# First stage of a hybrid encoder: the order of loads and stores on the sync queue around the memory's weights

## The chip, the core and the metric

The kernel is one program on one NeuronCore of a Trainium2 chip. The metric is the device time of one execution in microseconds (us). TensorE (PE) multiplies, VectorE (DVE), ScalarE (ACT) and GpSimd (POOL) do the rest, and all loads and stores are issued by SyncE (SP), one after the other, in one queue. SP's instructions are transfers ("DMA"), which run on 16 DMA engines.

## What is computed

One encoder layer over two sequences of 512 tokens (1024 channels), each with its own memory of 256 rows. What bears on the first stage:

```
xn = rmsnorm(x) * norm_mix                       # per token, both sequences
mn = rmsnorm(mem) * norm_mem                     # per memory row
mk, mv = split(mn @ w_mem_kv)                    # keys and values, 4 heads of 128
h  = xn @ w_in                                   # u, q, k, v, xq and three gates
```

`u` feeds a state-space scan (S5) over 512 tokens in 32 groups of 64 complex states, whose coefficients are computed from `lambda`, `log_step`, `b` and `c`. Then come attention over the tokens, attention over the memory, three gated merges, an output product and a gated feed-forward network. Everything is float32.

## The kernel before

**Products.** A float32 product is done as three products of rounded operands (`mm3`, L121 to L132; the same triple is written out for the values at L250 to L252). Each operand is split into a rounded high part and the rest: `split` (L103) makes the high part on ACT (L109 or L112) and the low part on DVE (L110 or L113). A weight tile is 128x1024 (512 KB). `weight` (L115) loads it into a buffer `wf` (L117), and splits it into `wh` (ACT, L109) and `wl` (DVE, L110). All three names have two buffers, so the load of a weight tile waits until DVE has made `wl` of the weight two before it, and its split waits until PE has finished with the weight two before it.

**First stage.** It computes the memory's keys and values and, beside them, everything that the products with `w_in` need.

- `mem_part` (L193) loads a quarter of the transposed memory (`mt`, L195) and splits it with `norm_mem` as scale (`mh`, `ml`).
- `mem_k` (L227) takes one head's key weight and does 8 x `mm3` into one PSUM bank: 24 matmuls of 512 columns. ACT copies the result to `mf` (L235), and after two heads `mf` is stored to `mD` in HBM (L237).
- `mem_v` (L241) loads one of four value weights and does 24 matmuls on four open banks (L250 to L252). After the last, ACT copies the banks (L278) and `mf` is stored (L279).
- `sums` (L199) loads four tiles of 128 token rows (`tk<-in_xN`, L204) and squares them on ACT with a sum over the row (L205).
- `x_load` (L211) loads the transposed tokens of one sequence in four pieces (`xt<-in_xT`, L213).
- `factor` (L165) takes the root on ACT (L169, which needs another ACT table than the copies), the reciprocal on DVE (L170), and spreads the result over the partitions by four PE transposes (L173).
- `x_norm` (L215) scales the eight pieces of a sequence on DVE (L220), and splits them: ACT makes `xh` (L221), DVE makes `xl` (L222).
- `s5_gen` (L907 on) is a generator: each `next(s5)` traces another part of the scan's work. The part in this stage loads `br`, `bi`, `cr`, `cn` (L927 to L930), computes powers of complex numbers on DVE (L891 to L1013, some hundred small operations), spreads them by ACT copies (L1022 to L1032), and forms products of 128x1024 on DVE (L1048 to L1050) that PE transposes (L1062).

**What sets the order.** The program is traced in the order of the source, and then a list scheduler places the instructions of every engine by its own estimate of when they become ready. Each engine then runs its own instructions strictly in the placed order. A DMA waits for the one eight places ahead of it on SP to have landed (eight semaphores are used in turn), and for its buffer. `tc.issue_after(ins)` is a scheduling edge: what a block traces on the engine of `ins` is queued behind `ins`. It carries no semaphore.

In the source before, the first stage reads: `mem_part(0)`, first key weight, the other `mem_part`s, S5 part, second key weight, `mem_k(0)`, third key weight, `mem_k(1)`, `sums` and `x_load` of the first sequence, fourth key weight, `mem_k(2)`, `x_norm(0)`, `sums` and `x_load` of the second sequence, `mem_k(3)`, `mem_v(0)`, `x_norm(1)`, `mem_v(1)` to `mem_v(3)`. Then follow the first products with `w_in` (the "u products", L281 to L296), gates and the S5 scan.

Of the kernel before, what the change touches and what calls it, by code (L numbers as in the profile page):

```python
# [10 lines left out]
F32 = mybir.dt.float32  # L11
# [8 lines left out]
P = 128  # L20
# [28 lines left out]
def encoder(ctx: ExitStack, tc: tile.TileContext, a, out):  # L49
    nc = tc.nc  # L50
# [8 lines left out]
    rp = ctx.enter_context(tc.tile_pool(name="rp", bufs=2))  # L59
# [21 lines left out]
    def slot(tag, shape=(P, NT), dt=F32, name="sl"):  # L81
        return pools[tag].tile(list(shape), dt, tag=tag, name=name)

    def bank(tag="mm"):
        return pools[tag].tile([P, 512], F32, tag=tag, name="bk" + tag)

    def aux():
        return bank("tr")
# [12 lines left out]
    def vcol(name, i=0):  # L101
        o = VEC[name][0] + i
        return vec[:, o : o + 1]  # L103


    def split(hi, lo, src, scale=None):

        if scale is None:
            S.copy(hi, src)  # L109
            V.tensor_tensor(out=lo, in0=src, in1=hi.bitcast(F32), op=ALU.subtract)  # L110
        else:
            S.activation(out=hi, in_=src, func=AF.Copy, scale=scale)  # L112
            V.scalar_tensor_tensor(out=lo, in0=src, scalar=scale, in1=hi.bitcast(F32), op0=ALU.mult, op1=ALU.subtract)  # L113

    def weight(src, n=DM, tag=None):  # L115
        wf = wp.tile([P, DM], F32, tag="wf", name="wf")
        nc.sync.dma_start(wf[:, :n], src)  # L117
        wh, wl = (slot(tag, dt=F32R, name=n_) if tag else wp.tile([P, DM], F32R, tag=n_, name=n_) for n_ in ("wh", "wl"))
        split(wh[:, :n], wl[:, :n], wf[:, :n])
        return wh, wl  # L120
# [3 lines left out]
    def mm3(outs, wh, wl, xs, k, nk):  # L124

        nonlocal last_mm
        ws = slice(k * P, (k + 1) * P)
        for s, (xh, xl) in enumerate(xs):
            PE.matmul(outs[s], wh[:, ws], xh, start=(k == 0), stop=False)  # L129
            PE.matmul(outs[s], wh[:, ws], xl, start=False, stop=False)  # L130
        for s, (xh, xl) in enumerate(xs):
            last_mm = PE.matmul(outs[s], wl[:, ws], xh, start=False, stop=(k == nk - 1))  # L132

    def proj(src, hi, lo, nk=KD, seqs=(0, 1)):


        wh, wl = weight(src, nk * P)
        outs = []
        for s in seqs:
            cs = slice(s * L, (s + 1) * L)  # L140
            outs.append(bank())
            for k in range(nk):
                mm3(outs[-1:], wh, wl, [(hi[k][:, cs], lo[k][:, cs])], k, nk)
        return outs
# [21 lines left out]
    def factor(ss, n, nt=4):  # L166

        rs = rp.tile([P, 4], F32, tag="rs", name="rs", bufs=4)
        S.activation(out=rs[:, :nt], in_=ss[:, :nt], func=AF.Sqrt, scale=1.0 / n, bias=epsc)  # L169
        V.reciprocal(rs[:, :nt], rs[:, :nt])  # L170
        bc = aux()
        for t in range(nt):
            PE.transpose(bc[:, t * P : (t + 1) * P], rs[:, t : t + 1].broadcast_to([P, P]), ident)  # L173
        return rs, bc
# [6 lines left out]
    mD = drp.tile([4, P, 2, L], F32, name="mD")  # L181
# [4 lines left out]
    s5 = s5_gen(kx)  # L186
# [6 lines left out]
    def mem_part(i):  # L193
        mt_ = slot("ld", [P, 2, L], name="mt")
        nc.sync.dma_start(mt_, a["memT"][:, 2 * i : 2 * i + 2, :])  # L195
        for j in range(2):
            split(mh[i][:, j, :], ml[i][:, j, :], mt_[:, j, :], scale=vcol("norm_mem", 2 * i + j))

    def sums(src, tag="wb"):  # L199

        ss = rp.tile([P, 4], F32, tag="ss", name="ss", bufs=3)
        for t in range(4):
            tk = slot(tag, [P, DM], name="tk")
            nc.sync.dma_start(tk, src[t])  # L204
            S.activation(out=tk, in_=tk, func=AF.Square, accum_out=ss[:, t : t + 1])  # L205
        return ss
# [1 line left out]
    xt = [slot("su", [P, KD, L], name="xt0"), [slot("wb", [P, 2, L], name="xt1") for _ in range(4)]]  # L208
    xt = [[xt[0][:, k] for k in range(KD)], [xt[1][k // 2][:, k % 2] for k in range(KD)], xt[0], xt[1]]

    def x_load(s):  # L211
        for i in range(4):
            nc.sync.dma_start(xt[2][:, 2 * i : 2 * i + 2] if s == 0 else xt[3][i], a["xT"][s, :, 2 * i : 2 * i + 2, :])  # L213

    def x_norm(s, ss):  # L215
        cs = slice(s * L, (s + 1) * L)
        _, bc = factor(ss, DM)
        for k in range(KD):
            x_ = xt[s][k]
            V.scalar_tensor_tensor(out=x_, in0=x_, scalar=vcol("norm_mix", k), in1=bc, op0=ALU.mult, op1=ALU.mult)  # L220
            S.copy(xh[k][:, cs], x_)  # L221
            V.tensor_tensor(out=xl[k][:, cs], in0=x_, in1=xh[k].bitcast(F32)[:, cs], op=ALU.subtract)  # L222
# [3 lines left out]
    mf = None  # L226

    def mem_k(h, w):
        nonlocal mf
        o = aux()  # L230
        for i in range(KD):
            mm3([o], *w, [(mhk[i], mlk[i])], i, KD)
        if h % 2 == 0:
            mf = slot("ld", [P, 2, L], name="mf")
        S.copy(mf[:, h % 2], o)  # L235
        if h % 2 == 1:
            nc.sync.dma_start(mD[h // 2], mf)  # L237

    ob = []

    def mem_v(c):  # L241
        wh, wl = weight(a["w_mv"][c])
        if c == 0:
            ob.extend(bank() for _ in range(4))
        for kk in range(2):
            kt = 2 * c + kk
            wsl = slice(kk * L, kk * L + L)
            for i in range(4):
                tk = slice(i * P, (i + 1) * P)
                PE.matmul(ob[i], mhk[kt][:, tk], wh[:, wsl], start=(kt == 0), stop=False)  # L250
                PE.matmul(ob[i], mhk[kt][:, tk], wl[:, wsl], start=False, stop=False)
                PE.matmul(ob[i], mlk[kt][:, tk], wh[:, wsl], start=False, stop=(kt == KD - 1))  # L252

    mem_part(0)
    mw = [weight(a["w_mk"][0])]
    for i in range(1, 4):
        mem_part(i)
    next(s5)
    mw.append(weight(a["w_mk"][1]))
    mem_k(0, mw[0])  # L260
    mw.append(weight(a["w_mk"][2]))
    mem_k(1, mw[1])
    ss = sums(a["xN"][0])
    x_load(0)
    mw.append(weight(a["w_mk"][3]))
    mem_k(2, mw[2])
    x_norm(0, ss)
    ss = sums(a["xN"][1])
    x_load(1)
    mem_k(3, mw[3])  # L270
    mem_v(0)
    x_norm(1, ss)
    for c in range(1, 4):
        mem_v(c)
    for s in range(NS):
        mf = slot("ld", [P, 2, L], name="mf")
        for j in range(2):
# [65 lines left out]
    with behind():  # L343

        mrs = cst.tile([P, 4], F32, name="mrs")
        mbc = cst.tile([P, L], F32, name="mbc")
        rs_, bc = factor(sums(a["memN"], "ld"), DM)
        V.tensor_copy(mrs, rs_)
        S.copy(mbc, bc)
# [355 lines left out]
    for i in range(3):  # L705
        for m in (i, i + 4):
            x1[m] = slot("x1", name=f"x1_{m}")
            w = weight(a["w_out"][m])
# [59 lines left out]
    for i in range(KFF):  # L768
        w = res0
        if i > 0:  # L770
            wg = weights4(i)
            w = next(wg)
# [53 lines left out]
    for bi, nb in enumerate(FBLK):  # L826
# [10 lines left out]
        for parts in (((0, L),), ((L, L // 2),), ((L + L // 2, L // 2),)) if last else (((0, L), (L, L)),):  # L837
            acc = new_acc() if last else None
            for m in range(KD):
# [9 lines left out]
                if not last:  # L849
                    wh, wl = weight(wsrc, nb * P)  # L850
                elif m in kept:
                    wh, wl = kept[m]
# [416 lines left out]
```

## Time and profile before

| | |
|---|---|
| time, median of 3 runs | 1673.69 us (1670.11 to 1674.54) |
| profiled execution, its own time | 1674.95 us |
| span of the profiled execution | 1673.2 us |
| PE busy | 97% of the span |
| DVE busy | 64% |
| ACT busy | 37% |
| DMA | 197.69 MB, mean 118 GB/s |

The profile is of one execution, and times in it count from the start of its span. A row of the timeline gives start and duration in us, engine, line of the source, operation, output and input, count, and in brackets the idle time of the engine ahead of it and what ended that. A row of the windows gives the busy time (and number of instructions) of PE, PE's weight loads, DVE, ACT and POOL in a stretch, the TensorE clock granted (1.00 is full), the share of the DMA engines' time and the rate. Consecutive matmuls overlap in the records: the distance from start to start is what one costs.

### The profile page before, as it was taken

To read this page: it belongs to the slowest core of one execution; us is meant where nothing else is said; L and a number is where in the kernel's file an instruction comes from. 1 tells how busy PE (TensorE), PEld (TensorE's weight loads), DVE (VectorE), ACT (ScalarE), POOL (GpSimd) and SP (SyncE) were. 2 spreads that over 40 slices of the span, in tenths; PEclk is the share of its full clock that TensorE was granted. 3 is DMA by queue.
4 is the path that set the end of the run, shared out by engine and by line. 5 is a ranking of instruction groups with operands and counts; after the bars stand their busy time and mean duration, and the time that the engine had idled before them with its cause. 6 is when DMAs were issued, how large, how long until landed. Compare 5 with 4: busy or idle time off the path is not lost.

```text
span 1673.2 us, 21052 instructions
## 1 busy us (share of the span) xinstructions
PE 1625.6 (97%) x7916; PEld 1357.8 (81%) x7916; DVE 1076.2 (64%) x1788; ACT 622.1 (37%) x1092; POOL 391.7 (23%) x253
## 2 busy tenths in 40 slices
PE   5999999999999999999999999999999999999997
PEld 4788887888897788878888878888888888888887
DVE  7946898154554776777655668777777777743324
ACT  6534412245343456554323443223323223421121
POOL 0001000000001121120243346555554552500021
PEclk9999999999999999999999999999999999999999
DMA  9343252747111221333554432322222223741302
GB/s 367 114 154 127 96 170 89 222 174 241 46 57 64 88 57 40 112 107 120 182 187 127 140 101 79 125 87 82 83 86 79 88 79 115 252 133 52 84 17 101
DMA packets 79269, 197.69 MB, mean 118 GB/s; under 512 B 11072, under 2 KB 26688, under 8 KB 79168
## 3 DMA queue, kind: packets, MB, share of 16 engines
q1 hardware_dynamic: 79168, 196.35, 35.4%
q8 instruction: 62, 1.02, 0.3%
q14 instruction: 39, 0.32, 0.1%
HBM read 141.82 MB, written 50.30 MB: 115 GB/s over the span
## 4 chain that ended last, share of the span: by engine, by line
PE 79%; DVE 11%; DMA 3%; issue 2%; ACT 2%; POOL 1%; SPq 1%; DVEq 0%; POOLq 0%; ACTq 0%
PE bkmm L129 15%; PE bkmm L132 15%; PE bkmm L130 15%; PE bkmm L738 8%; PE bkmm L737 8%; PE bkmm L739 8%; DVE st L1140 1%; DVE wl L110 1%; PE bktr L1122 1%; POOL mg L587 1%; PE bksc L533 1%; DMA c_n<-cD 1%; PE bksc L534 1%; PE bkmm L438 1%; PE bkmm L439 1%
## 5 line engine op out<-in xcount | busy, mean ns | idle before, releaser
L109 ACT CAST wh<-wf 128x1024 fp32r<-128x1024 f32 (+4 forms) x164 | 142.3, 868 | 385.4 <-PE bkmm L130 225.9
L132 PE MATMUL bkmm<-xh,wl 128*128 128x512 f32 x640 | 252.1, 394 | 3.0 <-DVE wl L110 3.0
L129 PE MATMUL bkmm<-xh,wh 128*128 128x512 f32 x640 | 251.8, 393 | 2.3 <-DVE t L505 1.2
L130 PE MATMUL bkmm<-xl,wh 128*128 128x512 f32 x640 | 251.7, 393 | 0.0
L738 PE MATMUL bkmm<-tl,wh 128*128 128x512 f32 x612 | 240.1, 392 | 2.5 <-DVE tl L110 2.5
L737 PE MATMUL bkmm<-th,wh 128*128 128x512 f32 x612 | 239.9, 392 | 0.0
L739 PE MATMUL bkmm<-th,wl 128*128 128x512 f32 x612 | 238.5, 391 | 0.0
L110 DVE TENSOR_TENSOR wl<-wf,wh 128x1024 fp32r<-128x1024 f32 (+4 forms) x164 | 175.7, 1072 | 94.5 <-ACT wh L109 93.9
L129 PE MATMUL bkmm<-ah,wh 128*128 128x512 f32 (+1 forms) x408 | 147.1, 361 | 0.2 <-ACT wh L109 0.2
L130 PE MATMUL bkmm<-al,wh 128*128 128x512 f32 (+1 forms) x408 | 147.0, 360 | 0.0
L132 PEld LDWEIGHTS bkmm<-xh,wl 128*128 128x128 f32 x640 | 120.7, 189 | 29.1 <-DVE wl L110 3.8
L129 PEld LDWEIGHTS bkmm<-xh,wh 128*128 128x128 f32 x640 | 120.7, 189 | 28.7 <-DVE t L505 2.6
L130 PEld LDWEIGHTS bkmm<-xl,wh 128*128 128x128 f32 x640 | 120.5, 188 | 24.7 <-issue 0.4
L506 POOL TENSOR_TENSOR t<-t,rs 128x512 f32<-128x512 f32 x16 | 24.6, 1537 | 494.5 <-DVE t L505 494.5
L738 PEld LDWEIGHTS bkmm<-tl,wh 128*128 128x128 f32 x612 | 115.8, 189 | 28.1 <-DVE tl L110 4.2
L737 PEld LDWEIGHTS bkmm<-th,wh 128*128 128x128 f32 x612 | 115.8, 189 | 24.4 <-ACT th L109 0.3
L739 PEld LDWEIGHTS bkmm<-th,wl 128*128 128x128 f32 x612 | 115.5, 189 | 24.0
L132 PE MATMUL bkmm<-ah,wl 128*128 128x512 f32 (+1 forms) x408 | 127.4, 360 | 0.5 <-DVE wl L110 0.4
L802 POOL TENSOR_TENSOR up<-up,acc 128x512 f32<-128x512 f32 x44 | 85.1, 1957 | 149.4 <-DVE up L778 149.4
L862 DVE TENSOR_TENSOR y<-y,bkmm 128x512 f32<-128x512 f32 (+1 forms) x56 | 32.6, 608 | 111.4 <-PE bkmm L132 111.4
L153 POOL TENSOR_TENSOR acc<-acc,nsq 128x512 f32<-128x512 f32 (+1 forms) x32 | 38.0, 1187 | 241.2 <-ACT nsq L152 241.1
L132 PEld LDWEIGHTS bkmm<-ah,wl 128*128 128x128 f32 x408 | 76.9, 189 | 12.7 <-DVE wl L110 1.3
(585 smaller groups left out, 3272.3 us busy)
## 6 DMA issues: line engine op xcount, KB each, us to landing
wf<-in_w_in SPq DMA_DIRECT2D x40, 512.0 KB, 3.8
gD<-gt SPq DMA_DIRECT2D x24, 512.0 KB, 2.8
gl<-gD SPq DMA_DIRECT2D x24, 512.0 KB, 3.9
wf<-in_w_fg SPq DMA_DIRECT2D x22, 512.0 KB, 3.7
wf<-in_w_fu SPq DMA_DIRECT2D x22, 512.0 KB, 3.7
aD<-ac SPq DMA_DIRECT2D x22, 512.0 KB, 2.6
fl<-aD SPq DMA_DIRECT2D x22, 512.0 KB, 4.5
wf<-in_w_fo SPq DMA_DIRECT2D x16, 448.0 KB, 3.3
```

Of the source, the lines that this page charges most:

```text
L109: S.copy(hi, src)
L110: V.tensor_tensor(out=lo, in0=src, in1=hi.bitcast(F32), op=ALU.subtract)
L129: PE.matmul(outs[s], wh[:, ws], xh, start=(k == 0), stop=False)
L130: PE.matmul(outs[s], wh[:, ws], xl, start=False, stop=False)
L132: last_mm = PE.matmul(outs[s], wl[:, ws], xh, start=False, stop=(k == nk - 1))
L153: eng.tensor_tensor(out=acc[:, :n], in0=acc[:, :n], in1=sq[:, :n], op=ALU.add)
L506: PO.tensor_tensor(out=t2, in0=t2, in1=rope[1], op=ALU.mult)
L737: PE.matmul(ps, wh[:, ws_], th[:, o], start=(k == 0), stop=False)
L738: PE.matmul(ps, wh[:, ws_], tl[:, o], start=False, stop=False)
L739: PE.matmul(ps, wl[:, ws_], th[:, o], start=False, stop=(k == 3))
L802: PO.tensor_tensor(out=up, in0=up, in1=accs[s], op=ALU.mult)
L862: V.tensor_tensor(out=y[m][:, c : c + n], in0=y[m][:, c : c + n], in1=o_, op=ALU.add)
```

## The change

Loads and stores of the first stage are tied behind loads of the memory's weights. `weight` remembers its last load, and blocks `with queued():` put what they trace on SP behind that load. The weights of the values are loaded where the source calls `weight`, ahead of the `mem_v` that uses them, and no longer inside it. `sums` and `x_load` can be traced in parts. The two stores of the keys leave `mem_k` and stand behind the load of the last value weight.

```diff
+    last_w = None
+
     def weight(src, n=DM, tag=None):
+        nonlocal last_w
         wf = wp.tile([P, DM], F32, tag="wf", name="wf")
-        nc.sync.dma_start(wf[:, :n], src)
+        last_w = nc.sync.dma_start(wf[:, :n], src)
...
-    def sums(src, tag="wb"):
+    def sums(src, tag="wb", ss=None, ts=range(4)):
...
-    def x_load(s):
-        for i in range(4):
+    def x_load(s, ts=range(4)):
+        for i in ts:
...
         S.copy(mf[:, h % 2], o)
-        if h % 2 == 1:
-            nc.sync.dma_start(mD[h // 2], mf)
+        return mf
...
-    def mem_v(c):
-        wh, wl = weight(a["w_mv"][c])
+    def mem_v(c, w):
+        wh, wl = w
...
+    def queued():
+
+        return tc.issue_after(last_w.ins)
+
     mem_part(0)
     mw = [weight(a["w_mk"][0])]
     for i in range(1, 4):
         mem_part(i)
-    next(s5)
     mw.append(weight(a["w_mk"][1]))
+    with queued():
+        next(s5)
+        ss0 = sums(a["xN"][0], ts=range(3))
     mem_k(0, mw[0])
     mw.append(weight(a["w_mk"][2]))
-    mem_k(1, mw[1])
-    ss = sums(a["xN"][0])
-    x_load(0)
+    with queued():
+        sums(a["xN"][0], ss=ss0, ts=(3,))
+        x_load(0, range(2))
+    mf0 = mem_k(1, mw[1])
     mw.append(weight(a["w_mk"][3]))
+    with queued():
+        x_load(0, range(2, 4))
+        ss1 = sums(a["xN"][1], ts=range(1))
     mem_k(2, mw[2])
-    x_norm(0, ss)
-    ss = sums(a["xN"][1])
-    x_load(1)
-    mem_k(3, mw[3])
-    mem_v(0)
-    x_norm(1, ss)
-    for c in range(1, 4):
-        mem_v(c)
+    mw.append(weight(a["w_mv"][0]))
+    x_norm(0, ss0)
+    with queued():
+        sums(a["xN"][1], ss=ss1, ts=range(1, 4))
+    mf1 = mem_k(3, mw[3])
+    mw.append(weight(a["w_mv"][1]))
+    with queued():
+        x_load(1)
+    mem_v(0, mw[4])
+    mw.append(weight(a["w_mv"][2]))
+    mem_v(1, mw[5])
+    mw.append(weight(a["w_mv"][3]))
+    with queued():
+        nc.sync.dma_start(mD[0], mf0)
+        nc.sync.dma_start(mD[1], mf1)
+    x_norm(1, ss1)
+    mem_v(2, mw[6])
+    mem_v(3, mw[7])
```

As built, SP's order before is: four `mt` with the first key weight among them, three small tables, second key weight, four token rows, one piece of x, third key weight, three pieces of x, two token rows, `br` to `cn`, fourth key weight, two token rows, two pieces of x, store of keys, first value weight, two pieces of x, second value weight, store of keys, the last two value weights. As built after: `mt` and first key weight, second key weight, three small tables, three token rows, `br`, `bi`, third key weight, one token row, two pieces of x, `cr`, `cn`, fourth key weight, two pieces of x, one token row, first value weight, three token rows, second value weight, four pieces of x, the last two value weights, both stores of keys.

More of the change, by code (lines that the diff above doesn't have):

```diff
@@ L197, in mem_part @@
             split(mh[i][:, j, :], ml[i][:, j, :], mt_[:, j, :], scale=vcol("norm_mem", 2 * i + j))
-    def sums(src, tag="wb"):
-        ss = rp.tile([P, 4], F32, tag="ss", name="ss", bufs=3)
-        for t in range(4):
+    def sums(src, tag="wb", ss=None, ts=range(4)):
+        if ss is None:
+            ss = rp.tile([P, 4], F32, tag="ss", name="ss", bufs=3)
+        for t in ts:
             tk = slot(tag, [P, DM], name="tk")
```

## Prediction

> **What bounds the kernel now.** I read the page's busy table first, then the windows by stage, then the timeline of each engine in the first 72 us.
>
> ```profile
> PE 1625.6 (97%) x7916; PEld 1357.8 (81%) x7916; DVE 1076.2 (64%) x1788; ACT 622.1 (37%) x1092; POOL 391.7 (23%) x253
> ```
>
> ```profile
> 22.00:46.50 24.50, 15.83 (x57) 11.87 (x58) 24.02 (x85) 17.37 (x40) 0.00 (x0) 0.79 0.79 313
> 60.00:265.00 205.00, 203.95 (x1040) 169.88 (x1038) 154.45 (x282) 68.40 (x140) 11.21 (x23) 1.00 0.39 132
> 545.00:820.00 275.00, 266.46 (x1423) 223.79 (x1422) 200.76 (x400) 149.15 (x330) 45.12 (x29) 1.00 0.31 98
> ```
>
> PE sets the time: 97% busy, and from 60 us on nearly without gaps. So a gap closed early moves all that follows. The stage of the change is where PE is not full: between 22 and 46.5 us it is busy for 15.8 of 24.5 us, at a granted clock of 0.79, while DVE is busy for 24.0. The gaps, on PE's timeline:
>
> ```profile
> 21.48 0.39 PE L132 MATMUL bktr<-mh,wl 128*128 128x512 f32 x1
> ...
> 25.68 0.50 PE L132 MATMUL bktr<-mh,wl 128*128 128x512 f32 x1 [1.02 <-DVE wl L110]
> ...
> 30.57 0.39 PE L132 MATMUL bktr<-mh,wl 128*128 128x512 f32 x1
> 34.86 0.79 PE L129 MATMUL bktr<-mh,wh 128*128 128x512 f32 x1 [3.90 <-ACT wh L109]
> ...
> 38.34 0.79 PE L132 MATMUL bktr<-mh,wl 128*128 128x512 f32 x1 [2.26 <-DVE wl L110]
> ...
> 46.01 0.60 PE L173 MATMUL bktr<-ident,rs 128*128 128x128 f32 x4
> ...
> 54.58 0.50 PE L251 MATMUL bkmm<-wl,mh 128*128 128x512 f32 x1 [1.25 <-DVE wl L110]
> ...
> 70.13 1.04 PE L1062 MATMUL bktr<-ident,cxr 128*128 128x128 f32 x8
> ...
> 71.47 0.40 PE L132 MATMUL bkmm<-xh,wl 128*128 128x512 f32 x1
> ```
>
> `mem_k(2)` starts late (its third matmul at 25.68), `mem_k(3)` later still (third matmul 38.34); one more gap of 1.25 us is at `mem_v(1)`. A matmul costs (30.57 - 25.68) / 21 = 0.23 us; after the long gap the 22 up to 46.01 took 7.67 us, 2.6 more than at that pace. Each wait ends in a split by ACT (L109) or DVE (L110), not in a load.
>
> **The loads.**
>
> ```profile
> 4.00:33.00 29.00, 20.10 (x76) 15.14 (x76) 23.72 (x89) 21.50 (x35) 0.00 (x0) 1.00 1.03 412
> ```
>
> ```profile
> 11.74 0.36 SPq L117 DMA_DIRECT2D wf<-in_w_mk  x1
> ```
>
> ```profile
> wf<-in_w_mk SPq DMA_DIRECT2D x1, 512.0 KB, 8.0
> ```
>
> The last two are the load of the third key weight, its issue and, alone in its window, its 8.0 us to landing: 19.7. At 412 GB/s 512 KB take 1.27 us. Before it stood eleven tiles of that size, now ten (three token rows, `br` and `bi`, no piece of x): it lands at about 18.5. The fourth key weight has 15 ahead where it had 19, and lands at about 25. But before, the third weight was cast only at 22.39:
>
> ```profile
> 16.47 0.59 ACT L235 COPY mf<-bktr 128x512 f32<-128x512 f32 x1 [1.75 <-PE bktr L132]
> ...
> 19.04 1.05 ACT L205 ACTIVATE tk<-tk 128x1024 f32<-128x1024 f32 x1
> ...
> 20.20 1.28 ACT L169 ACT_TABLE_LOAD   x1
> 21.49 0.30 ACT L169 ACTIVATE rs<-ss,epsc 128x4 f32<-128x4 f32 x1
> 21.91 0.59 ACT L235 COPY mf<-bktr 128x512 f32<-128x512 f32 x1
> 22.39 1.05 ACT L109 CAST wh<-wf 128x1024 fp32r<-128x1024 f32 x1
> ```
>
> It stood on ACT behind three squares, the table load, the root and the copy of `mem_k(1)`. So the order of the loads acts here through the placed order on ACT and DVE, and that I follow in the order as built.
>
> **The change, step by step.**
>
> *1. `mem_k(2)`.* After the copy at 16.47 ACT now has two squares (1.05 each), then the cast: 17.05 + 2.1 = 19.1 (landed 18.5), done 20.15. DVE makes `wl` behind some eleven small operations, 21.0 to 22.2. PE needs it at 21.9 + 0.45 = 22.3, so `mem_k(2)` follows `mem_k(1)` and ends at 21.9 + 24 x 0.23 = 27.4. Gained so far: 3.4 us.
>
> *2. A new wait on DVE.*
>
> ```profile
> 21.82 0.18 DVE L170 RECIPROCAL rs<-rs 128x4 f32<-128x4 f32 x1 [2.20 <-ACT rs L169]
> ...
> 22.39 0.18 DVE L966 SCALAR_TENSOR_TENSOR sh<-sh,h 128x32 f32<-128x32 f32 x1
> ...
> 24.41 1.21 DVE L110 TENSOR_TENSOR wl<-wf,wh 128x1024 fp32r<-128x1024 f32 x1
> ...
> 25.86 2.71 DVE L220 SCALAR_TENSOR_TENSOR xt<-xt,vec,bktr 128x512 f32<-128x512 f32 x4
> ...
> 37.08 1.21 DVE L110 TENSOR_TENSOR wl<-wf,wh 128x1024 fp32r<-128x1024 f32 x1
> 38.21 0.18 DVE L987 TENSOR_TENSOR ta<-pr,pi 128x32 f32<-128x32 f32 x1
> ...
> 42.99 0.68 DVE L985 TENSOR_TENSOR tb<-bi,gi 128x512 f32<-128x512 f32 x1
> ...
> 46.29 1.23 DVE L110 TENSOR_TENSOR wl<-wf,wh 128x1024 fp32r<-128x1024 f32 x1
> 47.43 5.35 DVE L220 SCALAR_TENSOR_TENSOR xt<-xt,vec,bktr 128x512 f32<-128x512 f32 x8
> ...
> 54.44 3.69 DVE L222 TENSOR_TENSOR xl<-xt,xh 128x512 fp32r<-128x512 f32 x6
> ...
> 64.88 1.22 DVE L1049 TENSOR_TENSOR cxr<-b_i,qi 128x1024 f32<-128x1024 f32 x1 [2.14 <-PE bkmm L252]
> 66.02 1.22 DVE L110 TENSOR_TENSOR wl<-wf,wh 128x1024 fp32r<-128x1024 f32 x1
> ```
>
> The fourth square of the first sequence now stands on ACT behind the copy of `mem_k(1)`, which PE ends at 21.9: copy to 22.4, square to 23.5, table to 24.8, root to 25.15. DVE's reciprocal, at 21.82 before, is at 25.2. As built DVE reaches it after `wl` (22.2) and six small operations (0.6), so it waits 2.4 us, about as long as before but later (ends: 0, and 3.0 if the six ran ahead). All of DVE is queued behind it, the split of the fourth key weight too.
>
> *3. `mem_k(3)`.* As built there follow 34 small operations, four scalings of x and then `wl`. Twenty small ones took 24.41 - 22.39 = 2.0 us (0.10 each), the 24 of the powers from 38.21 to 42.99 took 0.20 each. Some 22 of the first kind, 11 of the second and one 128x512 (0.4): 4.9 us, to 30.2. The scalings (2.7) end at 32.9, `wl` at 34.1. So the third matmul of `mem_k(3)` is at about 34.15 against 38.34: 4.2 us gained, no more, although the weight is cast at 26. PE stands idle from 28.3 to 34.15, longer in one piece than before (3.9 and 2.3), so I keep the slow pace: 7.67 us, end at 41.8.
>
> [...]
>
> *4. `mem_v(0)` and `mem_v(1)`.* DVE, from 34.1: four more scalings, five `xl` (0.6 each), three of the powers (0.3 each), then `wl` of the first value weight at 40.5 to 41.65, before PE comes (41.8). For the second, the buffer is free at 41.8; `wl` from about 43.9 to 45.0, needed at 48. The wait of 1.25 us at 54.58 goes. `mem_v(1)` ends at 41.8 + 5.7 + 5.5 = 52.9.
>
> *5. What is late next: DVE, up to the u products.* From 45.0: reciprocal, one `xl` and small ones to 46.6; six products for `b_r`, `b_i` (five took 46.29 - 42.99 = 3.3) to 50.6; `wl` of the third value weight to 51.75; one 128x1024 product to 52.9. The scalings of the second sequence need the transposes (L173), which PE now does behind `mem_v(1)`: 53.3, a wait of 0.5. Eight scalings (5.3) to 58.6; `wl` of the fourth value weight to 59.8, where PE, at `mem_v(3)` from 58.7, waits about 0.3; five `xl`, one product, one `xl` to 64.55; `wl` of the first `w_in` weight to 65.7. PE ends `mem_v(3)` at 64.4, is ready for the third u matmul at 64.85 and gets it at 65.7. Before it came at 71.47, with eight transposes (0.8 to 0.9 us) ahead of it that now stand behind. **Gain: 71.47 - 0.87 - 65.7 = 4.9 us.**
>
> The same from the other end: before, DVE worked from the reciprocal (21.82) to that `wl` (end 67.2) with 2.14 idle, 43.2 us of work. Now 2.4 of it (`wl`, a dozen small ones) is done ahead of the reciprocal and 1.2 (two `xl`) behind that `wl`: 39.6, and 25.2 + 39.6 + 0.5 = 65.3. So 4.9 to 5.3; I take the walk.
>
> *6. The queues.* Removed: the store of keys that blocked SP.
>
> ```profile
> SPq L237 <- ACT mf L235: 8.7, 1, 8.7
> ```
>
> ```profile
> L398 SPq DMA_DIRECT2D mt<-mD x4: 319/322/535, 388.0 to 394.3; - x4
> ```
>
> The store stood until 47.4 ahead of the third value weight, but the buffer of that load is free only when `wl` at 46.29 is done, 47.5: worth nothing. The moved stores are read after 388 us: nothing. Added: the load of the second value weight waits for `wl` of the fourth key weight (34.1), and behind it on SP stand the four pieces of the second sequence, of which two wait for squares as well (to 39.4). With the 8.0 us of a loaded queue they land by 48, needed at 53.3: hidden, with 5 us to spare; beyond that each us is a us on the walk. The last value weights, issued at 41.7 and 45, have 8 us and more until DVE comes to their `wl` (50.6 and 58.6). Ends: 0 to +3; I take 0.
>
> *7. After the stage.* The u products lose DVE's slack (4.3 us between 67.2 and 71.47, now none), but DVE is then ahead of PE: twelve 128x1024 products end near 85, and the next weight is due at 92. In the scan's preparation DVE waits for PE:
>
> ```profile
> 114.64 1.23 DVE L110 TENSOR_TENSOR wl<-wf,wh 128x1024 fp32r<-128x1024 f32 x1 [13.96 <-ACT wh L109]
> ...
> 180.99 0.69 DVE L1126 COPY st<-bktr 64x504 f32<-64x504 f32 x1 [1.83 <-ACT st L1125]
> ```
>
> The last copy ahead of the scan comes by ACT from PE, so the scan moves up with PE. Up to 545 us PE's order as built is the same as before; between 545 and 820 us (attention) the scheduler interleaves score products and projections otherwise, and after that it is the same again. PE idles 275.0 - 266.5 = 8.5 us there, most of it score products waiting for exponentials:
>
> ```profile
>   ACT e L371: 6.7, 10
> ```
>
> ```profile
> PE bksc L533 <- ACT e L371: 2.3, 4, 1.5
> ```
>
> (PE and its weight loads together, then PE alone: us, times, longest.) The new order has 18 score pairs with fewer than two other matmuls ahead, the old 19. Ends: -8.5 (no idle left) to +15 (ten waits of 1.5); I take 0, as the counts are nearly equal.
>
> **The sum** on the profiled execution is 1674.95 - 4.9 = 1670.1. That execution was 1.3 above the median of the runs shown, so the predicted time is 1673.7 - 4.9 = **1668.8 us**; with attention within 1.5 us either way, 1667.2 to 1670.4.
>
> **The rivals.**
>
> *DVE does not wait.* If the reciprocal cost no 2.4 us, all behind it would be as much earlier: gain 7.3, 1666.4. For it: nothing but x needs it. Against: it waited 2.20 in the same place before.
>
> *Attention falls better.* Idle from 8.5 to 5: gain 8.4, 1665.3. For it: one run of score pairs that waited now has more projections ahead. Against: nothing tied there was changed. *Attention falls worse*, by 3: 1671.7.
>
> *Slower.* One mechanism: at L533 a score product waits for the exponential that frees its bank, up to 1.5 us. Four such waits more eat the gain; from seven on the kernel is slower by over 0.3%. Eight: 1673.7 - 4.9 + 12 = 1681. Against: the counts of step 7.
>
> *It doesn't arrive.* If DVE reached the scan on its own chain and not through PE, the gaps in front of the gates would take the gain back: 1673.7. Against: the waits of 13.96 and 1.83 us.
>
> **How the numbers follow.** Forecast 0.50; DVE does not wait 0.06; attention better 0.15, worse 0.17; slower 0.05; not arriving 0.07. A difference of 0.3% is 5.0 us, about what a measurement of this kernel can tell from none; it lies at 1668.7, inside the forecast, of which I put 0.22 below. Faster: 0.22 + 0.06 + 0.15 = 0.43; slower 0.05; same 0.28 + 0.17 + 0.07 = 0.52. The range 1664.5 to 1673.8 leaves out the slower case and a third of the better attention, 0.1; narrower than that it would lose the case that does not arrive or the bounds of steps 5 to 7.
>
> **What would show it.** Step 1: no gap on PE at 22 us. Step 2: DVE's reciprocal near 25.2 with some 2.4 us idle. Step 3: PE idle from about 28 to 34 us, ended by L110, and a clock below 1 after it. Steps 4 and 5: no wait in the first two `mem_v`, waits under 1 us at the fourth and at the first u product, whose third matmul is near 65.7. Step 7: idle near 8.5 us in attention. A reciprocal well before 25, pieces of x that end a wait, or a wait at the scan would make it wrong.

## The result, and the profile after

| | before | after |
|---|---|---|
| median | 1673.93 us (11 runs, 1670.11 to 1676.45) | 1677.58 us (11 runs, 1675.12 to 1680.31) |
| profiled execution, its span | 1674.95, 1673.2 us | 1679.33, 1677.6 us |

The ratio is 1.0021, with a 95% interval of 1.0012 to 1.0031: 3.65 us slower, where 4.9 us faster was forecast.

The first stage came out as forecast. PE's timeline of the kernel after (start, duration, engine, line, operation, in brackets the idle time ahead and what ended it):

```profile
34.53 0.80 PE L135 MATMUL bktr<-mh,wl 128*128 128x512 f32 x1 [5.83 <-DVE wl L110]
...
59.96 0.50 PE L254 MATMUL bkmm<-wl,mh 128*128 128x512 f32 x1 [0.90 <-DVE wl L110]
...
65.85 0.50 PE L135 MATMUL bkmm<-xh,wl 128*128 128x512 f32 x1 [0.56 <-DVE wl L110]
```

and DVE's:

```profile
20.93 1.22 DVE L110 TENSOR_TENSOR wl<-wf,wh 128x1024 fp32r<-128x1024 f32 x1
...
25.67 0.18 DVE L173 RECIPROCAL rs<-rs 128x4 f32<-128x4 f32 x1 [2.90 <-ACT rs L172]
```

The third u matmul is at 65.85 (65.7 was forecast), and the lead over before is 71.47 - 0.87 - 65.85 = 4.75 us (0.87 is for the eight transposes that stand ahead of it only in the kernel before). The lead is still there when attention starts. The first score product, before and then after:

```profile
554.34 0.47 PE L533 MATMUL bksc<-m,m 128*128 128x512 f32 x1 [0.92 <-DMA m<-m]
...
652.84 0.50 PE L129 MATMUL bkmm<-xh,wh 128*128 128x512 f32 x1 [1.03 <-DVE vl L110]
...
654.79 0.39 PE L132 MATMUL bkmm<-xh,wl 128*128 128x512 f32 x1
```

```profile
549.89 0.47 PE L556 MATMUL bksc<-m,m 128*128 128x512 f32 x1 [1.02 <-DMA m<-m]
...
623.30 0.50 PE L556 MATMUL bksc<-m,m 128*128 128x512 f32 x1 [0.95 <-ACT e L394]
625.75 1.09 PE L176 MATMUL bktr<-ident,rs 128*128 128x128 f32 x4 [1.72 <-DVE rs L173]
...
652.26 0.80 PE L132 MATMUL bkmm<-xh,wh 128*128 128x512 f32 x1 [3.40 <-DVE vl L110]
...
655.76 0.40 PE L135 MATMUL bkmm<-xh,wl 128*128 128x512 f32 x1
```

Read the two fences against each other. 554.34 - 549.89 = 4.45 us of lead. The rows at 652.84 and 652.26 are the same matmul, the first of the projection that follows the second set of values: 0.58 is left. The rows at 654.79 and 655.76 are again one matmul, the ninth of that projection: now the kernel after is 0.97 us late, because those nine ran slowly. The clock says so. Windows of the kernel after (length, busy time of PE, its weight loads, DVE, ACT, POOL, then the granted clock, DMA share and rate):

```profile
545.00:820.00 275.00, 261.78 (x1376) 220.25 (x1375) 198.11 (x392) 143.40 (x317) 39.36 (x27) 0.98 0.30 96
...
625.00:630.00 5.00, 4.25 (x20) 4.28 (x21) 2.37 (x5) 3.15 (x7) 0.00 (x0) 0.50 0.14 52
630.00:635.00 5.00, 5.00 (x36) 4.91 (x35) 3.37 (x8) 1.86 (x6) 0.00 (x0) 0.82 0.01 3
...
650.00:655.00 5.00, 2.74 (x7) 2.17 (x8) 2.19 (x6) 3.60 (x14) 0.00 (x0) 0.72 0.32 105
655.00:660.00 5.00, 5.00 (x26) 4.21 (x25) 0.75 (x1) 0.40 (x1) 0.00 (x0) 0.94 0.00 0
```

PE idles 275 - 261.78 = 13.2 us in attention (8.5 before): 4.7 more. And where before had a clock of 1.00, four windows here lie below it. The clock of a window is a mean over its time, and a slow stretch runs at half the clock (0.50 in the first of them), so the slow time in a window is twice what its clock lacks: 5.0, 1.8, 2.8 and 0.6 us. PE is busy in 4.25, 1.8, 2.74 and 0.6 us of it, and half of that is lost: 4.7 us. Together 9.4, and 1674.95 - 4.75 + 9.4 = 1679.6, where the execution took 1679.33. What PE waited for in attention, kernel after (us in total, times, longest):

```profile
PE bkmm L132 <- DVE vl L110: 3.4, 1, 3.4
...
PE bksc L556 <- ACT e L394: 1.2, 2, 1.0
```

The largest is new in size: a projection (L132) waits for the low part of the values (`vl`, L110), which frees the banks that the projection needs.

### The profile page after: what moved, and what is told of

The parts are those of the page before. It is cut to its first block, busy times and chain, and to the rows that moved or that the text cites. A ratio compares the mean times of both kernels' runs of the same rounds, so it can differ in the third digit from the quotient of the medians.

```text
span 1677.6 us, 21042 instructions
## 1 busy us (share of the span) xinstructions
PE 1625.9 (97%) x7916; PEld 1360.0 (81%) x7916; DVE 1081.4 (64%) x1788; ACT 621.1 (37%) x1092; POOL 393.2 (23%) x253
## 4 chain that ended last, share of the span: by engine, by line
PE 83%; DVE 10%; DMA 2%; ACT 2%; issue 1%; POOL 1%; SPq 0%; DVEq 0%; POOLq 0%; ACTq 0%
PE bkmm L132 16%; PE bkmm L135 16%; PE bkmm L133 16%; PE bkmm L761 8%; PE bkmm L760 8%; PE bkmm L762 8%; DVE st L1163 1%; DVE wl L110 1%; PE bktr L1145 1%; PE bkmm L461 1%; PE bkmm L463 1%; PE bkmm L462 1%; PE bksc L556 1%; PE bksc L557 1%; PE bktr L565 1%
## 5 line engine op out<-in xcount | busy, mean ns | idle before, releaser
L132 PE MATMUL bkmm<-xh,wh 128*128 128x512 f32 x640 | 252.4, 394 | 3.5 <-DVE vl L110 3.4
L110 DVE TENSOR_TENSOR wl<-wf,wh 128x1024 fp32r<-128x1024 f32 (+4 forms) x164 | 176.8, 1078 | 93.5 <-ACT wh L109 92.2
L132 PE MATMUL bkmm<-ah,wh 128*128 128x512 f32 (+1 forms) x408 | 147.1, 361 | 0.1
L132 PEld LDWEIGHTS bkmm<-xh,wh 128*128 128x128 f32 x640 | 120.9, 189 | 29.1 <-DVE vl L110 3.9
```

## The experiments

Theory A: the scheduler interleaves attention otherwise, and that order is worse by some 8 us whatever stands ahead. Theory B: the lead is lost at something that comes at its own time, and the order only follows. To tell them apart, the order of one kernel was put on another. Everything traced from the scan on is the same list of instructions in both kernels, so order-only edges (the kind that `tc.issue_after` sets) can tie each instruction of an engine behind the one that precedes it in the wanted order. `ORDER` holds the numbers of the instructions of PE, DVE, ACT and SP in that order (GpSimd is left free).

```diff
+def pin(tc):
...
+    by = {i.name: i for i in tc.nc.cur_bb.bb.instructions}
+    for seq in ORDER.values():
+        last = None
+        for r in seq.split():
+            f, _, t = r.partition(":")
+            for n in range(int(f), int(t or f) + 1):
+                i = by["I-%d" % n]
+                if last is not None:
...
+                    tc.add_manual_dep(i, last, mybir.DependencyInfo(mybir.DependencyClass.NoSync, mybir.DependencyReason.DATA), reason="pin")
+                last = i.name
...
         encoder(tc, a, out)
+        pin(tc)
```

| run | first stage | attention order | median us | ratio to before (95%) |
|---|---|---|---|---|
| e1 | after | before | 1669.28 | 0.9970 (0.9958 to 0.9982) |
| e2 | before | after | 1681.43 | 1.0049 (1.0035 to 1.0063) |
| e3 | after | before up to 660 us, then after | 1673.02 | 0.9995 (0.9986 to 1.0004) |
| e4 | after | after up to 660 us, then before | 1672.68 | 0.9988 (0.9979 to 0.9998) |
| e5 | after | after, splits of the values ahead | 1672.75 | 0.9988 (0.9979 to 0.9997) |
| e6a | after, reciprocal later | before | 1667.84 | 0.9963 (0.9951 to 0.9976) |
| e6c | after, weight split ahead | before | 1666.77 | 0.9959 (0.9947 to 0.9972) |
| e6b | both of these | before | 1668.64 | 0.9966 (0.9954 to 0.9979) |
| e7 | after, stores as before | before | 1668.15 | 0.9963 (0.9950 to 0.9977) |
| e8 | change for the first sequence only | before | 1677.03 | 1.0019 (1.0010 to 1.0028) |
| e9 | change with one load tied earlier | the scheduler's own | 1669.98 | 0.9983 (0.9973 to 0.9993) |

The kernel before had medians of 1673.55 to 1674.14 beside these runs.

**e1, e2: the two halves exchanged.**

> The changed kernel with its first stage, but from the scan on every instruction of PE, DVE, ACT and SP is tied into the order in which the kernel before has it. Theory A (the loss is the order in which the scheduler interleaves the attention): the 4.75 us gained by the third u matmul are kept to the end, 1673.9 - 4.75 = 1669.2 us, and PE idles about 8.5 us between 545 and 820 us instead of 13.2. Theory B (the lead is lost at something that comes at its own time, a load, a store or GpSimd, and the order only follows): 1673.9 to 1677.6, PE idle 13 or more.

> The reverse: the first stage of the kernel before, and from the scan on the order of the changed kernel. Theory A: the order costs 1677.6 - 1673.9 + 4.75 = 8.4 us whatever stands ahead of it: 1682.3 us. Theory B: without a lead nothing is lost, 1673.9 us.

e1 is at 1669.28 where A said 1669.2; the same third u matmul, and attention with 7.9 us of idle time:

```profile
65.88 0.50 PE L135 MATMUL bkmm<-xh,wl 128*128 128x512 f32 x1 [0.60 <-DVE wl L110]
```

```profile
545.00:820.00 275.00, 267.08 (x1428) 224.66 (x1427) 199.33 (x398) 148.24 (x329) 45.33 (x29) 1.00 0.31 101
```

e2 is at 1681.43 (A: 1682.3, B: 1673.9). So the first stage is worth -4.85 us with the one order of attention (1669.28 - 1674.13) and -3.85 with the other (1677.58 - 1681.43), and the order +7.3 (1681.43 - 1674.13) or +8.3 (1677.58 - 1669.28). The two add up within 1 us (the runs of e2 spread from 1679.51 to 1685.79), and B has fallen.

**e3, e4: where in attention.**

> The changed kernel, with the order of before only from the scan to the first projection behind the second set of values (about 660 us), its own order behind that. In the two traces PE's lead over the kernel before is 4.5 us at 546 us, -1.0 at 660 and -5.2 at 833. Theory A: the first 5.6 us come back: 1677.6 - 5.6 = 1672.0. If the cost sat behind 660 us alone: 1677.6. Theory B: 1677.6.

> The changed kernel with its own order up to about 660 us, and that of before behind it. Theory A: the 4.2 us between 660 and 833 us come back, less the 0.8 that the trace gives back after 833: 1673.4 to 1674.2. If the cost sat ahead of 660 us alone: 1677.6 - 0 = 1677.6. Theory B: 1677.6.

Both halves of attention carry a part: 4.6 us come back with the first, 4.9 with the second (8.3 with both, so the sum is 1.2 too long, within the spread of the runs). Each was forecast within 1.5 us. For the second half, compare the stretch from the ninth matmul of that projection to one matmul that both kernels reach behind it, at 833.06 us before and at 838.26 after. Before, then after:

```profile
654.79:833.06 178.27, 174.83 (x877) 145.04 (x876) 126.86 (x238) 90.88 (x196) 32.56 (x19) 1.00 0.38 121
```

```profile
655.76:838.26 182.50, 176.47 (x878) 144.86 (x876) 127.35 (x237) 89.93 (x194) 30.26 (x19) 1.00 0.35 115
```

The clock is full in both. Of the 4.2 us that after takes longer, 2.6 are idle time of PE (6.0 against 3.4), and 1.6 are longer busy time for the same matmuls in another order. What lengthens the busy time is not settled.

**e5: one wait taken away.** In the kernel after, PE ends the last matmul of the values at 648.4, does four transposes, and has nothing but the projection next. ACT meanwhile does this:

```profile
647.64 0.38 ACT L109 CAST vh<-bkmm 128x256 fp32r<-128x256 f32 x1
648.45 0.37 ACT L109 CAST vh<-bkmm 128x256 fp32r<-128x256 f32 x1 [0.43 <-PE bkmm L463]
648.72 1.05 ACT L109 CAST wh<-wf 128x1024 fp32r<-128x1024 f32 x1
...
651.34 0.68 ACT L109 CAST vh<-bkmm 128x256 fp32r<-128x256 f32 x2
```

Two of the four casts stand behind a weight cast, an exponential and four squares (the rows left out), though their data were there at 648.4. The edit moves them, and on DVE the two `vl`. The order as a sketch:

```diff
 ACT:  vh vh
+      vh vh
       wh(cast)  e(exponential)  squares x4
-      vh vh
       table load, root
 DVE:  vl vl
+      vl vl
       wl  r  r
-      vl vl
```

> The changed kernel in its own order, with one thing moved: at 649 us ACT casts the last two halves of the values (L109, vh) before the weight cast, the exponential and the four squares, and DVE makes their low parts (vl) before that of the weight. In the changed kernel PE idles 3.40 us at 652.26, ended by this vl, and then does eight matmuls at 0.43 us instead of 0.23. Theory A1 (PE waits there for two banks whose split stands late on ACT and DVE): the casts are done at 649.4, vl at 650.2, so the wait falls to 1.3 and the end to 1677.6 - 2.1 = 1675.5; as far as 1674.0 if the clock then stays up as well. Theory A2 (another operand ends the wait there, or the time is lost again at the next wait): 1677.6.

The median is 1672.75, 4.8 us less than the kernel after; 2.1 to 3.6 was forecast. The wait is as forecast:

```profile
648.66 0.50 PE L132 MATMUL bkmm<-xh,wh 128*128 128x512 f32 x1 [1.19 <-DVE vl L110]
```

3.40 became 1.19: 2.2 us. And the matmul took 0.50 instead of 0.80, and the granted clock from 645 to 655 us is 1.00: it did not fall. What that is worth is read from the first and the ninth matmul of this projection: 655.76 - 652.26 = 3.50 us lie between them in the kernel after, 654.79 - 652.84 = 1.95 at full clock before, so 1.55. That makes 3.8. The profiled executions differ by more, 1679.33 - 1673.83 = 5.5, because e5 also has a shorter slow stretch behind the 1.72 us wait (mean clock between 625 and 635 us 0.83, against 0.66 in the kernel after); that wait was not touched, and the last section shows where such stretches came. A2 has fallen.

**e6a, e6c, e6b: what bounds the first stage.** Two moves of single instructions on DVE, in the kernel of e1, sketched as the order on DVE.

```diff
 DVE:  ... small operations of the powers (to 22.5 us)
-      reciprocal
       26 small operations
+      reciprocal                       # e6a, e6b
       8 small operations
+      wl of the fourth key weight      # e6c, e6b
       four scalings of x
-      wl of the fourth key weight
```

> The kernel of the first experiment (first stage of the change, attention order of before), with DVE's reciprocal at 25.51 us placed 26 small operations later, so that DVE need not wait 3.00 us for the root. Theory A (DVE's chain sets the end of the first stage): PE's transposes of the result stand at 27.48 and end at 28.1, so DVE waits there 0.6 instead, 2.4 less: 1669.3 - 2.4 = 1666.9, third u matmul near 63.5. Theory C (what sets the end of the stage is PE with its gap and its slow clock, or the loads): third u matmul at 65.85 as it is, 1669.3.

> The kernel of the first experiment with another single move on DVE: the low part of the fourth key weight (33.10 to 34.32) is made ahead of the four scalings of x (30.46 to 33.17) and not behind them. PE's gap of 5.8 us ahead of the third matmul of the fourth head becomes 3.1. Theory A (DVE's chain sets the end of the stage): DVE has the same work ahead of the first u product, so 1669.3 and a third u matmul at 65.85; PE waits for DVE later on. Theory C (PE with its gap sets it): 1669.3 - 2.6 = 1666.7, third u matmul at 63.2.

> Both moves on DVE together, in the kernel of the first experiment: the reciprocal 26 small operations later and the low part of the fourth key weight ahead of the four scalings. The reciprocal alone brought 1.55 us at the third u matmul, because 0.78 of 2.33 went into a longer wait of DVE at 50.77 for PE's second value part; the other move brings PE there earlier by more than 2 us. Theory A (DVE's chain sets the end, and PE only through that wait): the 0.78 come back, third u matmul at 65.88 - 2.33 = 63.5, 1669.3 - 2.4 = 1666.9. Rival (PE's gap and slow clock set that wait whatever stands ahead): 64.3, 1667.8.

PE in e6c:

```profile
31.85 0.80 PE L135 MATMUL bktr<-mh,wl 128*128 128x512 f32 x1 [3.21 <-DVE wl L110]
...
66.13 0.50 PE L135 MATMUL bkmm<-xh,wl 128*128 128x512 f32 x1 [0.60 <-DVE wl L110]
```

PE's gap fell from 5.83 to 3.21 us, and the third u matmul did not come earlier (66.13 against 65.88). So DVE's chain sets the end of the stage and not PE's gap: theory A by the trace. The median of 1666.77, which is what theory C gave, is lower than e1's all the same; the two profiled executions differ elsewhere, in the clock (last section). In e6a, DVE and then PE:

```profile
28.12 2.73 DVE L224 SCALAR_TENSOR_TENSOR xt<-xt,vec,bktr 128x512 f32<-128x512 f32 x4 [0.61 <-PE bktr L176]
...
50.77 1.23 DVE L1071 TENSOR_TENSOR ct<-b_r,qr 128x1024 f32<-128x1024 f32 x1 [1.70 <-PE bkmm L255]
```

```profile
64.33 0.50 PE L135 MATMUL bkmm<-xh,wl 128*128 128x512 f32 x1 [0.60 <-DVE wl L110]
```

The wait of 3.00 became 0.61 as forecast, but the next place where DVE depends on PE (50.77) took 0.78 of it (a wait of 1.70 instead of 0.92): 65.88 - 64.33 = 1.55 us gained. (The medians differ by 1.4, but they can't tell such kernels apart, see the last section.) e6b was to bring these 0.78 back, and did not:

```profile
29.36 0.51 PE L135 MATMUL bktr<-mh,wl 128*128 128x512 f32 x1 [0.40 <-DVE wl L110]
...
37.29 1.21 PE L253 MATMUL bkmm<-wh,mh 128*128 128x512 f32 x4 [2.64 <-ACT wh L109]
...
64.81 0.50 PE L135 MATMUL bkmm<-xh,wl 128*128 128x512 f32 x1 [0.60 <-DVE wl L110]
```

The long gap of PE is gone (0.40 at 29.36), but PE then waits for ACT's cast of the first value weight (2.64 at 37.29), and the stage ends at 64.81. Both theories missed: the wait moved to a third engine.

**e7, e8: parts of the change.** e7 puts the two stores of the keys back behind their heads. e8 keeps the change only for the first sequence.

```diff
 e7, in mem_k:
+        if h % 2 == 1:
+            nc.sync.dma_start(mD[h // 2], mf)
...
-    with queued():
-        nc.sync.dma_start(mD[0], mf0)
-        nc.sync.dma_start(mD[1], mf1)
 e8, the lines that it adds:
+    nc.sync.dma_start(mD[0], mf0)
...
     x_norm(0, ss0)
+    ss1 = sums(a["xN"][1])
+    x_load(1)
     mf1 = mem_k(3, mw[3])
+    nc.sync.dma_start(mD[1], mf1)
+    mem_v(0, weight(a["w_mv"][0]))
     x_norm(1, ss1)
+    for c in range(1, 4):
+        mem_v(c, weight(a["w_mv"][c]))
```

> The kernel of the first experiment, with one part of the change undone: the two stores of the keys stand again behind their heads, so that SP waits at them for the copies of the second and fourth head. Step 6 of the prediction (the moved stores are worth nothing, as the loads behind them have several us in hand): third u matmul at 65.9 as in the first experiment, 1669.3. Rival (SP blocked at a store delays a value weight that DVE or ACT then waits for): third u matmul later by 1 us or more, 1670.3 or more.

> The change for the memory's keys alone: scan's loads, token rows and x of the first sequence are queued behind the key weights as in the change, but from the third head on the source is that of before (token rows and x of the second sequence not tied, the value weights loaded inside mem_v, the stores of the keys behind their heads). From the scan on the order of before, as in the first experiment. If the gain comes from what stands ahead of the third and fourth head alone: third u matmul within 0.5 of 65.85 and 1669.3. If the early value weights carry a part, the 1.25 us wait in the second value part returns and PE is at the third u matmul at 67 or later: 1670.5 or more.

In e7 the third u matmul is not late but 1.26 us early, because the scheduler also placed the first stage a little otherwise (the reciprocal waits 2.35 us, and 3.00 in e1). So the stores are not tested alone; but SP waits for the two copies for only 2.3 us in all, and neither ACT nor DVE waits for the load of a value weight:

```profile
64.62 0.51 PE L135 MATMUL bkmm<-xh,wl 128*128 128x512 f32 x1
```

e8 was far off: 1677.03, where 1669.3 or 1670.5 and more was expected. PE in e8:

```profile
33.12 0.80 PE L132 MATMUL bktr<-mh,wh 128*128 128x512 f32 x1 [5.19 <-ACT wh L109]
...
56.06 0.80 PE L254 MATMUL bkmm<-wl,mh 128*128 128x512 f32 x1 [4.28 <-DVE wl L110]
...
75.20 0.40 PE L135 MATMUL bkmm<-xh,wl 128*128 128x512 f32 x1
```

With the second sequence untied, ACT casts the fourth key weight only at 32.03, behind two of its squares and two pieces of x (25.70 in e1), and DVE makes the low part of the second value weight behind eight scalings (54.78). The third u matmul is at 75.20, 3.7 us later than before, and the median is 3.2 us above before. So the ties of the first sequence alone don't give the gain. e8 undoes the ties of the second sequence, the early loads of the value weights and the move of the stores together; the cast at 32.03 points at the second sequence, but the parts were not run one by one.

**e9: no order written out.**

```diff
     with queued():
         next(s5)
-        ss0 = sums(a["xN"][0], ts=range(3))
+        ss0 = sums(a["xN"][0])
     mem_k(0, mw[0])
     mw.append(weight(a["w_mk"][2]))
     with queued():
-        sums(a["xN"][0], ss=ss0, ts=(3,))
         x_load(0, range(2))
```

> No order is written out here: the source of the change with one line moved, so that the fourth tile of token rows of the first sequence is tied behind the second key weight like the other three, and not behind the third. The first stage should end as in the change within 1 us (third u matmul 64.9 to 66.9). But the scheduler then gives ACT the order of before around 650 us: two casts of the values ahead of the four squares and the third and fourth right behind, no weight cast between them. Theory A (the order of attention decides, and any small edit of the first stage throws it anew): 1669 us, 1667.5 to 1671, no wait of 3.4 us at the first projection behind the values. Theory B (the ties of the change cost what is lost): 1677.6.

1669.98 us (1667.20 to 1675.22), and the third u matmul is at 65.16. At the place of the 3.40 us wait:

```profile
644.65 0.50 PE L132 MATMUL bkmm<-xh,wh 128*128 128x512 f32 x1 [1.08 <-DVE vl L110]
```

ACT has three of the four casts ahead of the four squares there, the fourth behind them, and no weight cast between. One load tied to another weight at the start of the kernel gives attention an order without that wait, so the ties as such do not cost what the change lost. One such edit was tried; that any small edit throws the order anew is not shown.

## Why the prediction was wrong

- *Steps 1 and 2* were right: `wl` of the third key weight at 20.93 (21.0), no wait of PE there; the reciprocal at 25.67 with 2.90 us idle (25.2 and 2.4). e6a shows that this wait is worth 1.55 us and not the 2.4 of the rival "DVE does not wait".
- *Step 3* was right in its time (34.53 for 34.15). The slow spell behind it was shorter than priced: 22 matmuls took 6.65 us (the last starts at 40.95, one costs 0.23), not 7.67. It cost nothing, as DVE ends last there. From the row at 34.53 on the trace has seven matmuls at half speed (0.43 us from start to start, 0.59 for the first) and the eighth at the change, which starts 3.15 us later; the granted clock is 0.50 from 34.42 to 37.83 us and 1.00 from there to 41.25.
- *Steps 4 and 5* were right: no wait in the first two value parts, 0.90 at the fourth, 0.56 at the first u product, and 4.75 us gained for 4.9. e6c confirms that DVE binds.
- *Step 6* was right for the stores as far as e7 shows it: no wait for a value weight with the stores at their old place.
- *Step 7, first half*, was right: 4.45 us of the lead are at the first score product, so the rival "it doesn't arrive" is out.
- *Step 7, second half*, is the step that failed: "Ends: -8.5 (no idle left) to +15 (ten waits of 1.5); I take 0, as the counts are nearly equal." The order cost 7.3 to 8.3 us (e1, e2). The counts were of score products with too little ahead of them, because before waited most for exponentials. But the new waits are not there: score products waited 1.2 us for exponentials (2.3 before). The largest wait is of a projection for the split of the values, 3.40 us, and the order as built had shown it: on ACT two casts behind a weight cast and four squares, and on PE nothing between the last value matmul and the projection but four transposes. e5 shows that this place alone is worth 3.8 us in the traces, wait and slow clock together (the median fell by 4.8).
- The sum had no term for the clock in attention. The clock fell to 0.50 at the waits of 0.95 and 1.72 us around 625 us and again behind that of 3.40: 4.7 of the 9.4 us.
- Of the rivals, "attention falls worse" was right in kind; its 3 us should have been 7 to 8. "Slower" had the right side with the wrong mechanism. The range of 1664.5 to 1673.8 held e1's 1669.28, that is, the change with the order of attention left alone, and not the change as built.

## What to carry to other kernels

Where one list scheduler places the whole program, an edit can deal the order anew in a much later stage that has choices, and that can outweigh the edit: here -4.9 us at the place of the edit and +7 to +8 five hundred us later. So compare the order as built stage by stage, and in a stage that changed ask of each engine what now stands ahead of the instruction that frees a bank or a buffer, not only how the waits of the old order fare. To judge an edit by itself, tie the other stages into their old order; to keep its gain, do the same, or try a neighbouring edit (e9).

## What the runs showed of the hardware that was not expected

Whether a gap of 1.72 or of 3.40 us on PE took the clock down was not settled by its length. The same two gaps, in the same order of instructions, in e2 and e4. e2:

```profile
629.19 1.09 PE L173 MATMUL bktr<-ident,rs 128*128 128x128 f32 x4 [1.72 <-DVE rs L170]
...
654.25 0.50 PE L129 MATMUL bkmm<-xh,wh 128*128 128x512 f32 x1 [3.40 <-DVE vl L110]
```

e4:

```profile
623.05 0.62 PE L176 MATMUL bktr<-ident,rs 128*128 128x128 f32 x4 [1.72 <-DVE rs L173]
...
646.83 0.50 PE L132 MATMUL bkmm<-xh,wh 128*128 128x512 f32 x1 [3.40 <-DVE vl L110]
```

In e2 the four transposes behind 1.72 us took 1.09 (slow), and behind 3.40 the clock stayed full. In e4 it is the other way round: 0.62 (full) behind the short gap, and a fall behind the long one. In the kernel after it fell at both.

These rows go with where a gap lies on a grid of time. In the traces of both kernels the stretches at half clock, but for the one that runs past the program's end, begin and end on one grid of 3.413 us. In the kernel after they begin at 31.01, 529.35, 624.93, 652.23 and 1003.80 us, that is 146, 174, 182 and 285 steps of 3.413 us behind the first; they last one to three steps. In the kernel before they begin at 33.59, 279.35 and 996.15 us, 72 and 282 steps behind the first, and last one to four; the two grids lie 2.58 us apart. Here are windows of one such step each, e2 and then e4:

```profile
625.09:628.50 3.41, 1.43 (x8) 0.79 (x7) 0.99 (x4) 3.39 (x13) 0.00 (x0) 1.00 0.01 2
628.50:631.91 3.41, 2.72 (x13) 2.75 (x14) 1.81 (x5) 1.58 (x6) 0.00 (x0) 0.50 0.00 0
...
648.98:652.39 3.41, 1.87 (x15) 1.54 (x13) 1.94 (x4) 2.80 (x7) 0.00 (x0) 1.00 0.00 0
652.39:655.80 3.41, 1.55 (x7) 1.29 (x8) 1.77 (x6) 3.21 (x13) 0.00 (x0) 1.00 0.45 150
655.80:659.22 3.42, 3.42 (x18) 2.82 (x17) 0.04 (x1) 0.00 (x0) 0.00 (x0) 1.00 0.01 4
```

```profile
620.61:624.02 3.41, 1.69 (x11) 1.29 (x12) 2.17 (x8) 2.59 (x6) 0.00 (x0) 1.00 0.00 0
624.02:627.43 3.41, 3.41 (x31) 3.41 (x31) 1.71 (x4) 2.65 (x4) 0.00 (x0) 1.00 0.23 82
...
644.50:647.91 3.41, 1.08 (x5) 0.90 (x6) 2.10 (x5) 3.38 (x14) 0.00 (x0) 1.00 0.34 118
647.91:651.33 3.42, 3.42 (x10) 2.65 (x9) 0.18 (x1) 0.29 (x1) 0.00 (x0) 0.50 0.09 36
```

In e2 the gap of 0.95 us ahead of the 1.72 and the first part of the latter lie in one window: 3.41 - 1.43 = 1.98 us idle, and the clock is at 0.50 in the next. The gap of 3.40 us is cut in two by the grid, 1.54 and 1.86 us idle, and the clock stays. In e4 the window with the gap of 1.72 us has no more idle time than that, and the clock stays; most of the gap of 3.40 lies in one window (2.33 idle), and it falls. In the traces of both kernels, step by step of their grids from 14 us on, each of the seven windows at full clock with 1.85 us idle or more was followed by one at half clock. Of those with less, two of the kernel before (1.56 us idle at 992.73 and 1.55 at 1661.75) and one of the kernel after (0.97 at 1000.39) were too, while one of the kernel after with 1.67 (at 269.93) was not. What sets these apart is open.

So two kernels that run the same instructions in the same order differed by some 1.5 us at a place. e1, then e6c, which run the same order from the scan on and have the same two gaps here (1.0 and 0.89 us):

```profile
526.16:529.58 3.42, 1.53 (x8) 0.90 (x7) 2.52 (x6) 1.42 (x3) 0.00 (x0) 1.00 0.11 28
529.58:532.99 3.41, 3.41 (x10) 2.66 (x9) 0.62 (x1) 0.58 (x1) 2.54 (x2) 0.50 0.53 186
```

```profile
522.77:526.18 3.41, 2.40 (x14) 1.80 (x12) 0.57 (x1) 1.59 (x3) 0.00 (x0) 1.00 0.01 2
526.18:529.59 3.41, 2.52 (x9) 1.71 (x10) 2.58 (x6) 0.53 (x1) 0.70 (x1) 1.00 0.48 148
529.59:533.01 3.42, 3.42 (x16) 2.81 (x15) 0.73 (x2) 1.32 (x3) 1.88 (x2) 1.00 0.28 92
```

Both gaps fall into one window in e1 (1.89 us idle) and into two in e6c (1.01 and 0.90), and e1 alone has a slow stretch, as it has between 270 and 290 us (mean clock 0.91, against 1.00 in e6c). Matmul by matmul, e1 loses 1.5 us at each of the two. It gets 1.5 back by 543 us, where e6c waits twice for DVE (0.54 and 0.57), loses some 1.0 again up to 1004 us, and ends with a span 2.5 us longer (1667.5 against 1665.0). So medians of e1, e6a, e6b, e6c and e7 (1666.8 to 1669.3) do not rank these kernels; all five are faster than both kernels of the study, by 4.9 to 7.1 us against the runs of before beside them.
